# Log-sum-exp over heads: four batches share a turn and logarithm, two more another; one warming matmul per half unit; the last turn in another PSUM bank; the bias check read from the bias row

## The chip, the cores and the metric

The kernel runs on one core of one Trainium2 chip. The metric is the time of one execution on the device in microseconds; the median of three runs counts. A core has five engines with queues of their own: TensorE (PE in the profile, its weight loads PEld), VectorE (DVE), ScalarE (ACT), GpSimd (POOL) and SyncE (SP), which here issues nearly all transfers. Sixteen DMA engines move the data of all queues.

## The reference, cut to what matters

```python
def reference(x, bias):                       # x 8 x 2048 x 2048, bias 8 x 256
    B, S, D = x.shape
    H = bias.shape[0]
    Dh = D // H
    x_heads = x.reshape(B, S, H, Dh).transpose(0, 2, 1, 3)
    x_heads = x_heads + bias[None, :, None, :]
    x_tiled = np.repeat(x_heads, 2, axis=2)   # each row twice
    mx = x_tiled.max(axis=-1, keepdims=True)
    lse = mx.squeeze(-1) + np.log(np.exp(x_tiled - mx).sum(axis=-1))
    return lse.astype(np.float32)             # 8 x 8 x 4096
```

For each of 8 x 2048 rows and each of 8 heads of 256 columns, the bias is added, and the logarithm of the sum of the exponentials is written twice. The input has 134 MB, the output 1 MB.

## The kernel before

**Tiles.** A tile t (0 to 63, eight for each batch) is 256 rows: 128 partitions times K = 2 rows of 2048 columns, 2 MB. Eight tile buffers (`xts`, in pairs `xbs`) hold x and are overwritten in place. Loads go out from SP: tiles 2 to 41 in pairs (4 MB, line 180), the others one by one or, from tile 57 on, by half units of one row per partition (line 192). The last tile's two half units are loaded in column pieces (`LAST_COLS`): the second one as 0-512, 768-1280, 1280-1792, 512-768 and 1792-2048. A load waits until the last users (`last_uses`) of its buffer's earlier tile are done.

**The sums.** No maximum is taken: exp(x + bias) is summed as it stands. The heads of a tile are shared among the engines by the tile's stage (`STAGES`). In the bulk (tiles 0 to 53), the bias of heads 0 to 2 is put into PSUM by `put_bias` (line 312), x is added with an identity matmul (`late_heads`, line 371), and ACT takes the exponential from PSUM (lines 382 and 389); for the heads 4 to 7 POOL adds the bias in place (`g_add`, line 421) and ACT takes the exponential (line 427); head 3 gets its bias as a factor exp(bias) from DVE (line 439); DVE sums (line 446). From tile 57 on, ACT takes the exponential of x as it lands (line 427), DVE multiplies by exp(bias) and sums in one instruction (`weigh`, line 462), POOL folds one or two heads (lines 478 and 486) for a short DVE sum (line 492), and PE and ACT do one to three heads with the bias in PSUM (`put_bias` line 329, `add_x` line 347, `sum_biased` line 402). In each of these half units, 14 in all, `keep_warm` issues `NWARM` = 3 identity matmuls of 128 columns into `tp` (line 362).

**The bias for PE.** `put_bias` uses three matmuls with one row each (`bparts`) for the first `NEARLY` = 5 tiles, and one matmul with `b3`, which holds the parts in three partitions, for later ones. `b3` is filled by three small DMAs that ACT issues (line 239). `first_factors`, `other_factors` and lines 244 to 254 prepare the factors.

**The results.** The sums of batch b lie in a tile `Rx[b]` of 128 partitions with one column before and one behind for a running minimum and maximum. When a batch of the first six is done (two tiles later), `finish(b)` turns its sums with four PE transposes into the PSUM tile `tp` (line 506), and one ACT instruction takes the logarithm, twice per row, into `res` (line 516, 32 partitions). `ends_of(b)` lets DVE carry the smallest and largest sum on to the next tile `Rx[b + 1]` (lines 534 and 537). Behind tile 61 (`t == T - 3`), `turn_two` turns batch 6 into `tp` (line 618), and `store` issues one DMA with the results of the first six batches (line 520). Behind the last tile `finish_two` takes batch 6's logarithm (line 629) and stores it (line 630); `finish_last` turns batch 7 into another quarter of `tp` (line 637), takes the logarithm (line 643) and stores it (line 644). `tp` is one PSUM bank, and the framework keeps writes and reads of two engines in it apart.

**The check.** `b_far` is the largest absolute bias; past a limit, or where a sum has run out of range, `judge` (lines 553 to 562) gives a number that lets all engines branch into `all_again`, a slow exact version that does not run here. `begin_row` (line 547) and `judge` use a row of the PSUM tile `one_ps`.

**Order.** The order on each engine is that in which the program is written (`manual_schedule`); `for_pool` and `for_pe` hold work back for the next unit. Semaphores come from the framework, which derives waits from the operands; `on_x` and `on_bank` declare pairs that need none. DMA completions use a small set of semaphores in turn, so that an issue on SP can also wait for the landing of an earlier DMA.

Of the kernel before, what the change touches and what calls it, by code (L numbers as in the profile page):

```python
# [9 lines left out]
F32 = mybir.dt.float32  # L10
BF16 = mybir.dt.bfloat16
I32 = mybir.dt.int32
ACT = mybir.ActivationFunctionType
# [7 lines left out]

NBUF = 8

NEARLY = 5

NWARM = 3

# [27 lines left out]
    [(0, 512), (1280, 2048), (512, 1280)],  # L57
    [(0, 512), (768, 1280), (1280, 1792), (512, 768), (1792, 2048)],
]


@with_exitstack
def kernel(
# [35 lines left out]
    bparts = sb.tile([1, 3, CPE], BF16, name="bparts")  # L99
    brest = sb.tile([1, 2, CPE], F32, name="brest")  # L100

    b8 = sb.tile([H, Dh], F32, name="b8")
    b_far = sb.tile([H, 1], F32, name="b_far")
    ident_bf = sb.tile([P, P], BF16, name="ident_bf")
    one_bits = sb.tile([1, 1], BF16, name="one_bits")
    ends = sb.tile([P, 2], F32, name="ends")
# [2 lines left out]

    NR = KB * H * NB  # L110

    Rx = [sb.tile([P, 1 + NR + 1], F32, name=f"R{b}") for b in range(B)]
    R = [r[:, 1 : 1 + NR].rearrange("p (k h n) -> p k h n", k=KB, h=H) for r in Rx[:-2]]
    R.append(Rx[-2][:, 1 : 1 + NR].rearrange("p (k h n) -> p k h n", k=K, h=H))
    R_last = Rx[-1][:, 1 : 1 + NR].rearrange("p (h n k) -> p h n k", h=H, n=NBLK)
    res = sb.tile([H * NB, B - 2, P, KB, 2], F32, name="res")
    res_two = sb.tile([H * NBLK, P, K, 2], F32, name="res_two")
    res_last = sb.tile([P, P, 2], F32, name="res_last")
    xbs = [sb.tile([P, KB, D], F32, name=f"xb{i}") for i in range(NBUF // TB)]
# [12 lines left out]
    def pieces(t):  # L132

        if len(modes_of(t)) == 1:
            return [(0, K, 0, D)]
        cols = [[(0, D)]] * K if t < T - 1 else LAST_COLS
        return [(k, k + 1, c0, c1) for k in range(K) for c0, c1 in cols[k]]
# [35 lines left out]
    def load(t):  # L173
        if TB <= t < BLOCKS:

            if t % TB == 0:
                after = [u for i in range(TB) if t >= NBUF for u in last_uses[t + i - NBUF]]
                ins = on_x(
                    t,
                    nc.sync.dma_start(  # L180
                        out=xbs[t // TB % len(xbs)], in_=rows_of(t, TB)
                    ),
                    after,
                )
                for i in range(TB):
                    loads[t + i, 0, 0] = ins
            return
        after = last_uses[t - NBUF] if t >= NBUF else []
        for k0, k1, c0, c1 in pieces(t):
            loads[t, k0, c0] = on_x(  # L190
                t,
                nc.sync.dma_start(
                    out=xts[t % NBUF][:, k0:k1, c0:c1],
                    in_=rows_of(t)[:, k0:k1, c0:c1],
                ),
                after,
            )
# [21 lines left out]
            )  # L219
            break  # L220
    nc.scalar.dma_start(out=brow, in_=bias.rearrange("h j -> (h j)").unsqueeze(0))
    nc.scalar.dma_start(out=b8, in_=bias)
    for t in range(NBUF):
        load(t)
    nc.vector.memset(ones, 1.0)
# [22 lines left out]
    for i, c in enumerate(range(G0, D, MM)):  # L248
# [5 lines left out]
    nc.scalar.activation(out=w_late, in_=w_late, func=ACT.Exp)  # L254

    nc.vector.memset(Rx[0][:, 0:1], 1.0)
    nc.vector.memset(Rx[0][:, 1 + NR :], 1.0)
    nc.vector.memset(one_bits, float(ONE_BITS))
    nc.vector.tensor_reduce(
        out=b_far,  # L260
        in_=b8,
        op=ALU.max,
        axis=mybir.AxisListType.X,
        apply_absolute_value=True,
    )
    nc.vector.tensor_scalar(
        out=Rx[0][0:H, 1 + NR :],
        in0=b_far,
        scalar1=BIAS_MAX,
        scalar2=TOO_FAR,  # L270
# [87 lines left out]
        return heads  # L358

    def keep_warm():  # L360
        for _ in range(NWARM):
            nc.tensor.matmul(  # L362
                tp[:, 0], lhsT=ident, rhs=ident, start=True, stop=True
            )

    def late_heads(m, t, got, sums):

# [131 lines left out]

        return add_fold  # L500

    def finish(b):

        nr = H * NB
        for k in range(KB):
            nc.tensor.transpose(
                out=tp[0:nr, k],
                in_=R[b][:, k].rearrange("p h n -> p (h n)"),
                identity=ident,
            )  # L510
        tv = bass.AP(
            tensor=tp.tensor,
            offset=tp.offset,
            ap=[[tp.ap[0][0], nr], [1, P], [P, KB], [0, 2]],
        )
        nc.scalar.activation(out=res[:, b], in_=tv, func=ACT.Ln)  # L516

    def store():

        nc.sync.dma_start(  # L520
            out=out[0 : B - 2].rearrange("b h (n r) -> (h n) b r", n=NB),
            in_=res.rearrange("q b p k r -> q b (p k r)"),
        )

    def ends_of(b):


        bits = Rx[b].bitcast(I32)
        if b < B - 1:
            low = Rx[b + 1][:, 0:1].bitcast(I32)  # L530
            high = Rx[b + 1][:, 1 + NR :].bitcast(I32)
        else:
            low, high = ends[:, 0:1], ends[:, 1:2]
        nc.vector.tensor_reduce(
            out=high, in_=bits[:, 1:], op=ALU.max, axis=mybir.AxisListType.X
        )
        nc.vector.tensor_reduce(
            out=low,
            in_=bits[:, 0 : 1 + NR],
            op=ALU.min,  # L540
            axis=mybir.AxisListType.X,
            negate=b == B - 1,
        )

    def begin_row():
# [87 lines left out]
        )  # L633

    def finish_last():
        last = tp[:, KB - 1]
        nc.tensor.transpose(
            out=last, in_=R_last.rearrange("p h n k -> p (h n k)"), identity=ident
        )
        tv = bass.AP(  # L640
            tensor=last.tensor, offset=last.offset, ap=[last.ap[0], [1, P], [0, 2]]
        )
        nc.scalar.activation(out=res_last, in_=tv, func=ACT.Ln)
        nc.sync.dma_start(
            out=out[B - 1].rearrange("h (n r) -> (h n) r", r=2 * P),
            in_=res_last.rearrange("q p r -> q (p r)"),
        )
# [25 lines left out]
    def flush(later_work):  # L673
        for f in later_work:
            f()
        later_work.clear()

    for t in range(T):
        if t == T_FACTORS:
            other_factors()  # L680
        xt = xts[t % NBUF]
        sums = sums_of(t)
        for k0, k1, c0, c1 in pieces(t):
            m = modes_of(t)[k0]
            add = None
            heads = []
            if c0 == 0:
                bias_here = bias_there
            if m["late"]:
                pe_part = late_heads(m, t, bias_here, sums)  # L690
            else:
                heads = add_x(m, t, k0, c0, c1, bias_here)

                def pe_part(t=t, heads=heads, sums=sums):
                    for k, h, bank, p, mm in heads:
                        sum_biased(t, k, h, bank, p, mm, sums)

            if c0 == 0:
                if next_units and not m["late"]:
                    bias_there = put_bias(*next_units.pop(0))  # L700
                if t > T_PROMPT and m["g0"] == H:
                    keep_warm()
                if m["g0"] < H:
                    add = g_add(m, t, k0, k1)
                if t < T - 1 or k0 == 0:
                    flush(for_pool)
            h0 = max(c0 // Dh, m["pe"])
            h1 = min(c1 // Dh, m["g0"])
            hf = max(h0, min(h1, H - m["fold"]))
            if h0 < h1 and not m["late"]:  # L710
                done = exp_inplace(
                    t, xt[:, k0:k1, h0 * Dh : h1 * Dh], loads[t, k0, c0]
                )
                if hf < h1:
                    for_pool.append(fold(t, k0, hf, h1, sums, done))
            if c0 == 0:
                flush(for_pe)
            if not m["late"]:
                for k in range(k0, k1):
                    for h in range(h0, hf):  # L720
                        weigh(
                            t,
                            xt[:, k, h * Dh : (h + 1) * Dh],
                            h,
                            sums[:, k, h : h + 1],
                            done,
                        )

            def pool_part(t=t, m=m, k0=k0, k1=k1, sums=sums, add=add):
                if add:  # L730
                    later(m, t, k0, k1, sums, add)
                if k1 == K:
                    reload(t)

            for_pool.append(pool_part)
            if m["g0"] < H:
                pe_part()
                if t == T_PROMPT - 1:
                    first_factors()
                if m["late"]:  # L740
                    bias_there = put_bias(*next_units.pop(0))
            elif heads:
                for_pe.append(pe_part)

        fb, at = divmod(t - 2, NBLK)
        if 0 <= fb < B - 2 and at == NBLK - 1:
            finish(fb)
            ends_of(fb)
        if t == T - 3:
            turn_two()  # L750
            ends_of(B - 2)
            store()
    row = begin_row()
    flush(for_pe)
    flush(for_pool)
    finish_two()
    finish_last()
    ends_of(B - 1)
    again = judge(row) > SPAN_BITS

    order.__exit__(None, None, None)
# [32 lines left out]
```

## Time and profile before

| what | value |
|---|---|
| median of 3 runs | 326.29 us (326.26 to 326.46) |
| the profiled execution | 326.43 us, of which the span from first to last instruction is 324.5 us |
| busy share of the span | PE 77%, DVE 89%, ACT 82%, POOL 89% |
| x queue (q1), share of 16 DMA engines | 98.3% |
| HBM read, written | 134.23 MB, 1.05 MB |
| mean TensorE clock granted | 0.945 of full speed |

Shares are averages over stages that have different limits, so the stretches of time are to be read one by one. The times of lines come from one execution, which took 0.14 us more than the median.

### The profile page before, as it was taken

What the parts mean: (1) busy time and instruction counts of PE and PEld (TensorE: products, weight loads), DVE (VectorE), ACT (ScalarE), POOL (GpSimd) and SP (SyncE); (2) the same over time, 40 slices, a digit from 0 to 9 for tenths busy, and PEclk for the clock granted to TensorE, in tenths of its full rate; (3) what the DMA queues carried; (4) which work ended last, traced back from release to release, by engine and by line L of the source; (5) the groups of instructions that cost most, each with busy time, mean ns of one, the idle gap of its engine ahead of it and who ended that gap; (6) DMA issues with size and microseconds to landing.
All of it is one profiled execution on the core that took longest, in us unless ns stands there. A gap on an engine that the chain in (4) does not pass through costs nothing.

```text
span 324.5 us, 2454 instructions
## 1 busy us (share of the span) xinstructions
PE 250.7 (77%) x691; PEld 106.4 (33%) x691; DVE 287.9 (89%) x330; ACT 266.6 (82%) x426; POOL 287.9 (89%) x121
## 2 busy tenths in 40 slices
PE   5999998778776787777697786677778676398883
PEld 2333333333332233332233332233333322155451
DVE  1146679999999999999969999999999999999995
ACT  1157679899779878788869988889988989889995
POOL 7939998999999999999999999999999999958863
PEclk9977789999999899999879999999999999669999
DMA  7999999999999999999999999999999999999994
GB/s 305 469 392 452 448 402 441 440 420 432 440 420 429 434 428 428 444 424 421 448 421 422 444 428 420 420 430 432 422 424 429 428 425 426 415 421 418 418 397 133
DMA packets 8896, 135.45 MB, mean 417 GB/s; under 512 B 1065, under 2 KB 1457, under 8 KB 2481
## 3 DMA queue, kind: packets, MB, share of 16 engines
q1 hardware_dynamic: 8768, 135.27, 98.3%
q8 instruction: 5, 0.08, 0.1%
q14 instruction: 9, 0.07, 0.1%
q10 hardware_dynamic: 114, 0.02, 0.0%
HBM read 134.23 MB, written 1.05 MB: 417 GB/s over the span
## 4 chain that ended last, share of the span: by engine, by line
DMA 34%; DVE 26%; PE 16%; POOL 14%; ACT 9%; issue 0%; SPq 0%; DVEq 0%
DMA xb<-in_x_dram 33%; DVE R L446 20%; POOL xb L421 14%; PE pair L371 6%; ACT xb L427 6%; PE one_ps L371 4%; DVE xb L439 3%; PE pair L312 3%; DVE xb L462 2%; PE one_ps L312 1%; PE pair L244 1%; ACT xb L389 1%; DMA brow<-in_bias_dram 1%; ACT xb L382 1%; ACT res L516 0%
## 5 line engine op out<-in xcount | busy, mean ns | idle before, releaser
L421 POOL TENSOR_TENSOR xb<-xb,b_rep 128x2048 f32<-128x2048 f32 x57 | 257.5, 4541 | 21.0 <-DMA xb<-in_x_dram 21.0
L446 DVE TENSOR_REDUCE R<-xb 128x14 f32<-128x3584 f32 (+1 forms) x57 | 216.8, 3803 | 1.9
L427 ACT ACTIVATE xb<-xb 128x2560 f32<-128x2560 f32 (+5 forms) x77 | 157.4, 2055 | 17.7 <-POOL xb L421 17.0
L371 PE MATMUL pair<-xb,ident 128*128 128x512 f32 x216 | 110.3, 636 | 0.0
L371 PE MATMUL one_ps<-xb,ident 128*128 128x512 f32 x108 | 61.0, 648 | 13.8 <-DMA xb<-in_x_dram 13.8
L389 ACT ACTIVATE xb<-pair 128x1024 f32<-128x1024 f32 x54 | 55.4, 1026 | 18.1 <-PE pair L371 18.0
L371 PEld LDWEIGHTS pair<-xb,ident 128*128 128x128 f32 x216 | 44.3, 205 | 57.5 <-issue 57.5
L439 DVE TENSOR_TENSOR xb<-xb,w_ps 128x512 f32<-128x512 f32 x54 | 36.7, 680 | 23.9 <-ACT xb L427 23.9
L312 PE MATMUL one_ps<-b,ones_bf 128*128 128x512 bf16 x49 | 19.0, 387 | 37.9 <-ACT xb L382 37.8
L312 PEld LDWEIGHTS <-ones_bf 128*128 128x128 bf16 (+1 forms) x192 | 18.9, 100 | 89.6 <-issue 80.4
L382 ACT ACTIVATE xb<-one_ps 128x256 f32<-128x256 f32 x108 | 39.8, 377 | 6.3 <-PE one_ps L371 6.3
L347 PE MATMUL pair<-xb,ident 128*128 128x512 f32 (+1 forms) x36 | 20.7, 660 | 12.0 <-DMA xb<-in_x_dram 12.0
L312 PE MATMUL pair<-b,ones_bf 128*128 128x512 bf16 x98 | 29.2, 380 | 0.0
L371 PEld LDWEIGHTS one_ps<-xb,ident 128*128 128x128 f32 x108 | 19.2, 196 | 27.5 <-DMA xb<-in_x_dram 20.3
L462 DVE CUSTOM_DVE_ANT_0 xb<-xb,w_ps 128x256 f32<-128x256 f32 x61 | 22.3, 415 | 0.0
L382 ACT ACTIVATION_READ_ACCUMULATOR xb<-one_ps 128x1 f32 x108 | 22.0, 203 | 0.0
L486 POOL TENSOR_TENSOR xb<-xb 128x128 f32<-128x128 f32 (+3 forms) x39 | 13.9, 356 | 3.1
L478 POOL TENSOR_TENSOR xb<-xb,w_sb 128x256 f32<-128x256 f32 (+1 forms) x13 | 10.1, 774 | 5.4 <-ACT xb L427 5.1
L362 PEld LDWEIGHTS tp<-ident 128*128 128x128 f32 x84 | 12.0, 202 | 4.8 <-issue 4.2
L402 ACT ACTIVATE xb<-pair 128x256 f32<-128x256 f32 x33 | 12.5, 396 | 0.0
L362 PE MATMUL tp<-ident 128*128 128x128 f32 x84 | 12.3, 285 | 0.0
L347 PEld LDWEIGHTS pair<-xb,ident 128*128 128x128 f32 x36 | 5.9, 207 | 17.3 <-DMA xb<-in_x_dram 17.2
(60 smaller groups left out, 91.5 us busy)
## 6 DMA issues: line engine op xcount, KB each, us to landing
xb<-in_x_dram SPq DMA_DIRECT2D x20, 4096.0 KB, 21.5
xb<-in_x_dram SPq DMA_DIRECT2D x17, 2048.0 KB, 22.7
xb<-in_x_dram SPq DMA_DIRECT2D x12, 1024.0 KB, 23.4
xb<-in_x_dram SPq DMA_DIRECT2D x4, 256.0 KB, 13.8
xb<-in_x_dram SPq DMA_DIRECT2D x2, 384.0 KB, 15.9
out_dram<-res SPq DMA_DIRECT2D x1, 768.0 KB, 7.2
xb<-in_x_dram SPq DMA_DIRECT2D x2, 128.0 KB, 6.4
out_dram<-res_two SPq DMA_DIRECT2D x1, 128.0 KB, 2.5
```

The source lines that it names most:

```text
L312: nc.tensor.matmul(p, lhsT=lhsT, rhs=each_row(b, h * Dh, Dh, K), start=i == 0, stop=False,)
L347: mm = nc.tensor.matmul(p, lhsT=ident, rhs=xts[t % NBUF][:, ka:kb, c : c + w], start=False, stop=True,)
L362: nc.tensor.matmul(tp[:, 0], lhsT=ident, rhs=ident, start=True, stop=True)
L371: mm = nc.tensor.matmul(p, lhsT=ident, rhs=xts[t % NBUF][:, :, h * Dh : (h + 1) * Dh], start=False, stop=True,)
L382: act = nc.scalar.activation(out=xts[t % NBUF][:, k, 0:Dh], in_=got[0][:, k * Dh : (k + 1) * Dh], func=ACT.Exp, accum_out=sums[:, k, 0:1],)
L389: act = nc.scalar.activation(out=xts[t % NBUF][:, :, Dh : m["pe"] * Dh].rearrange("p k (h j) -> p h k j", j=Dh), in_=got[-1].rearrange("p ...
L421: add = nc.gpsimd.tensor_tensor(out=v, in0=v, in1=each_row(b_rep, c - G0, D - c, k1 - k0), op=ALU.add)
L427: return on_x(t, nc.scalar.activation(out=v, in_=v, func=ACT.Exp), [after])
L439: mul = nc.vector.tensor_tensor(out=f, in0=f, in1=each_row(w_ps, m["pe"] * Dh - W0, n, k1 - k0), op=ALU.mult,)
L446: red = nc.vector.tensor_reduce(out=sums[:, k0:k1, h0:H], in_=v.rearrange("p k (h j) -> p k h j", j=Dh), op=ALU.add, axis=mybir.AxisListTy ...
L462: ttr = nc.vector.tensor_tensor_reduce(out=v, in0=v, in1=w, scale=1.0, scalar=0.0, op0=ALU.mult, op1=ALU.add, accum_out=dst,)
L486: done = nc.gpsimd.tensor_tensor(out=v[:, :, 0:n], in0=v[:, :, 0:n], in1=v[:, :, n : 2 * n], op=ALU.add)
```

## The change

The results of the first six batches are kept in groups: four batches (128 partitions after the turn) and two (64). `finish(i)`, `ends_of(i)`, `Rx` and `res` now go by group, so that there are two turns of four transposes and two logarithms in place of six each, at tiles 33 and 49; `store` issues one DMA for each group. `keep_warm` is one matmul of 384 columns that reads `b_rep` and writes three quarters of `tp`. `turn_two` moves from tile 61 to behind the last tile's work. `finish_last` uses the next bank of `pairs` in place of a quarter of `tp`. The one-row form of the bias is used for two tiles, not five. `b_far` is taken from the bias row `brow` (1 partition of 2048), and the load of the 8 x 256 copy `b8` is gone. The last half unit's pieces 512-768 and 1792-2048 are loaded by one DMA.

```diff
-NEARLY = 5
-
-NWARM = 3
+NEARLY = 2
+
+WARM = 384
...
+LAST_BOTH = (512, 1792)
...
-    b8 = sb.tile([H, Dh], F32, name="b8")
-    b_far = sb.tile([H, 1], F32, name="b_far")
+    b_far = sb.tile([1, 1], F32, name="b_far")
...
+    starts = [0]
+    while starts[-1] < B - 2:
+        starts.append(min(starts[-1] + P // (H * NB), B - 2))
+    groups = list(zip(starts, starts[1:]))
+    widths = [(b1 - b0) * NR for b0, b1 in groups] + [NR, NR]
...
+            if t == T - 1 and k0 == K - 1 and c0 in LAST_BOTH:
+                if c0 == LAST_BOTH[0]:
+                    both = slice(0, None, (LAST_BOTH[1] - c0) // Dh)
+                    v = [
+                        a[:, k0, c0:D].rearrange("p (a j) -> p a j", j=Dh)[:, both]
+                        for a in (xts[t % NBUF], rows_of(t))
+                    ]
+                    ins = on_x(t, nc.sync.dma_start(out=v[0], in_=v[1]), after)
+                    for c in LAST_BOTH:
+                        loads[t, k0, c] = ins
+                continue
...
-    nc.scalar.dma_start(out=b8, in_=bias)
...
         out=b_far,
-        in_=b8,
+        in_=brow,
         op=ALU.max,
...
     def keep_warm():
-        for _ in range(NWARM):
-            nc.tensor.matmul(
-                tp[:, 0], lhsT=ident, rhs=ident, start=True, stop=True
-            )
+        nc.tensor.matmul(
+            tp[:, 0 : WARM // P], lhsT=ident, rhs=b_rep[:, 0:WARM], start=True, stop=True
+        )
...
-    def finish(b):
-
-        nr = H * NB
+    def finish(i):
+
+        nr = widths[i] // KB
         for k in range(KB):
             nc.tensor.transpose(
                 out=tp[0:nr, k],
-                in_=R[b][:, k].rearrange("p h n -> p (h n)"),
+                in_=sums_in[i][:, k * nr : (k + 1) * nr],
                 identity=ident,
             )
...
-        nc.scalar.activation(out=res[:, b], in_=tv, func=ACT.Ln)
+        nc.scalar.activation(out=res[i], in_=tv, func=ACT.Ln)
...
-        nc.sync.dma_start(
-            out=out[0 : B - 2].rearrange("b h (n r) -> (h n) b r", n=NB),
-            in_=res.rearrange("q b p k r -> q b (p k r)"),
-        )
+        for (b0, b1), r in zip(groups, res):
+            nc.sync.dma_start(
+                out=out[b0:b1].rearrange("b h (n r) -> (b h n) r", n=NB),
+                in_=r.rearrange("q p k r -> q (p k r)"),
+            )
...
     def finish_last():
-        last = tp[:, KB - 1]
-        nc.tensor.transpose(
+        bank = n_ps[0] % len(ps)
+        last = ps[bank][:, 0:P]
+        turn = nc.tensor.transpose(
             out=last, in_=R_last.rearrange("p h n k -> p (h n k)"), identity=ident
         )
+        on_bank(bank, turn)
...
-        nc.scalar.activation(out=res_last, in_=tv, func=ACT.Ln)
+        on_bank(bank, nc.scalar.activation(out=res_last, in_=tv, func=ACT.Ln))
...
-        fb, at = divmod(t - 2, NBLK)
-        if 0 <= fb < B - 2 and at == NBLK - 1:
-            finish(fb)
-            ends_of(fb)
+        for i, (_, b1) in enumerate(groups):
+            if t - 2 == b1 * NBLK - 1:
+                finish(i)
+                ends_of(i)
         if t == T - 3:
-            turn_two()
-            ends_of(B - 2)
+            ends_of(len(groups))
             store()
     row = begin_row()
     flush(for_pe)
     flush(for_pool)
+    turn_two()
     finish_two()
     finish_last()
-    ends_of(B - 1)
+    ends_of(len(groups) + 1)
     again = judge(row) > SPAN_BITS
```

## The prediction

> **What bounds the kernel now.** I read the page's slices and queues first, then busy time by stretches, then the chain of waits and the timeline of the last ten microseconds. All lines are of the kernel before.
>
> The page, slices and queues (the digits are tenths in 40 slices):
>
> ```profile
> DMA  7999999999999999999999999999999999999994
> ...
> q1 hardware_dynamic: 8768, 135.27, 98.3%
> ```
>
> The x queue keeps the 16 DMA engines busy from the second slice to the last but one. Is that so even where engines are full? Busy time by stretches:
>
> ```profile
> core 0: us, PE busy (x) PEld busy (x) DVE busy (x) ACT busy (x) POOL busy (x), PEclk, DMA share, GB/s
> 250.00:290.00 40.00, 27.63 (x68) 10.79 (x67) 39.79 (x48) 35.91 (x52) 35.74 (x8) 0.87 1.01 424
> 290.00:300.00 10.00, 8.69 (x44) 5.52 (x42) 10.00 (x49) 10.00 (x22) 8.09 (x18) 1.00 1.01 417
> 300.00:310.00 10.00, 8.15 (x38) 4.95 (x38) 10.00 (x61) 9.79 (x25) 8.21 (x19) 1.00 1.01 419
> 310.00:318.00 8.00, 6.61 (x37) 4.81 (x38) 7.29 (x44) 7.60 (x19) 5.96 (x14) 1.00 1.03 386
> ```
>
> DVE and ACT are full, yet the DMA share is 1.0; earlier stretches of 50 us are alike (424 to 434 GB/s). The page's issues land 21.5 to 23.4 us after their issue, so some 9 MB is always queued (22 us by 424 GB/s). A buffer given back a few us earlier or later changes nothing. Up to about 310 us the stream sets the time, and work taken from PE, ACT or DVE there is worth nothing. Then comes the tail. The chain of waits, in order of time:
>
> ```profile
> 292.89 19.93 DMA xb<-in_x_dram
> ...
> 312.85 1.71 ACT xb L427
> ...
> 319.91 0.14 DVE R L492
> ```
>
> The row of tile 62 that lands at 312.82 starts a DVE run that ends at 320.05. What follows shows in the timeline, and the one wait of SP's at the end:
>
> ```profile
> 319.77 0.60 ACT L629 ACTIVATE res_two<-tp 64x512 f32<-64x512 f32 x1
> 320.39 0.55 SPq L630 DMA_DIRECT2D out_dram<-res_two  x1
> 320.42 0.33 PE L637 MATMUL tp<-ident,R 128*128 128x128 f32 x1 [1.73 <-ACT res_two L629]
> 320.78 0.38 ACT L643 ACTIVATE res_last<-tp 128x256 f32<-128x256 f32 x1 [0.42 <-PE tp L637]
> 321.19 0.36 SPq L644 DMA_DIRECT2D out_dram<-res_last  x1
> ```
> ```profile
> SPq L789 <- DMA out_dram<-res_last: 0.5, 1, 0.5
> ```
>
> The last turn waits for the other logarithm's read of the same bank, not only for its sums (320.05). The last store lands 2.0 us after its issue (the page's issues list), at 323.2; SP had been waiting 0.5 us for it, since 322.7, when the check's branch was through. From 323.2 to the end at 324.5 nothing but closing semaphores runs.
>
> **The change part by part.** *Last turn in another bank.* Its sums are there at 320.05; with the 0.05 us that the chain shows from DVE to a next engine it runs 320.10 to 320.43. ACT is through with res_two at 320.37, so the last logarithm starts at 320.46 (320.78 is 0.03 behind the turn's end now) and ends at 320.84. SP could issue at 320.87, but its issue of res_two holds it from 320.39 to 320.94. So 320.94 for 321.19: 0.25 us earlier, landing at 322.94. Ends: 0, if the two stores (landing 2.5 and 2.0 us after issue) now hold each other up by as much, or if the turn still waits for ACT; 0.50, where SP's own arrival at 322.7 takes over. I take 0.25. The page "DMA: Bandwidth & Descriptors" of the Trainium skill (section Anatomy of one DMA) puts some 2.0 us of a transfer down to setup and receipt; an estimate from its fit is 2.3 us for 128 KB, within what the two stores show, and it leaves the sum as it is.
>
> *Two last loads in one.* The pieces were issued at 310.31 and 312.84 and landed so:
>
> ```profile
> xb<-in_x_dram SPq DMA_DIRECT2D x1, 128.0 KB, 7.5
> ...
> xb<-in_x_dram SPq DMA_DIRECT2D x1, 128.0 KB, 5.3
> ```
>
> That is 317.8 and 318.1. The bytes keep their place in the queue, so both columns now count as landed at 318.1. The first piece's matmul (0.70 us, x2, line 347) moves from 317.85 to 318.2 and ends at 318.9; ACT reads it at 319.41 behind other work. The last piece's exponential starts at about 318.4 behind others anyway. So nothing, with 0.5 us of cover. One issue (0.33 us) leaves SP.
>
> *Turn of batch 6 moved* behind the last matmul and line 547 (0.21 us): two transposes of 0.27 us, 319.1 to about 319.65, and the logarithm that reads them starts at 319.77, when ACT gets to it. Nothing, with 0.1 us of cover; without it 0 to 0.3 us, which passes to the end through ACT. Behind it on PE stand only the last turn (free at 320.10) and the check's matmul (320.88).
>
> *Stores.* Two issues (0.35 us each) for one; with the load that is gone SP has as many as before, at 312.84 and about 313.5, behind all loads in the same queue. SP then sat 5.9 us before line 630. Nothing.
>
> *Warming.* Three pairs of 128 columns took 0.83 us per half unit. A pair of 256 takes 0.70, one of 512 takes 1.02 to 1.13 (line 347), so 384 lies between, about 0.9: +0.07 us, bounds -0.13 and +0.30, in 14 half units of some 2.5 us each, of which PE is busy about 2.0. Covered by DMA; in the last one by the wait for the landing at 318.1. What it may do to the clock is a rival.
>
> *Shared turns and logarithms.* ACT loses four of six (1.01 us each, a width that does not change) and waits of 0.6 us (3.7 over six): 6.5 us. PE loses 16 of 24 transposes (0.27 us): 4.4. DVE goes from 8 pairs of end reductions (0.19 us each in the chain) to 4, of 514, 258, 130 and 130 columns; by line 446 (3.89 us for 3584 columns, 1.09 ns each) a 385-column rise adds 0.41 us and 129 add 0.14: 16 x 0.19 = 3.0 becomes 2.6. All before 256 us but the same last pairs, under a DMA share of 1.0: nothing. PE's transposes at tile 33 wait for DVE with the bulk's matmuls behind them, as each finish did (1.2 us at most).
>
> *One-row bias for two tiles.* Nine matmuls (2.0 us) become three (0.38 each) for three tiles: 2.7 us of PE between 23 and 43 us. b3's last DMA is issued at 9.0 and lands within 6.9 us, before 16; its first reader comes at 23.5. Nothing: the queue behind is full.
>
> *Check from the row.* The reduction goes from 0.40 us to that of 2048 elements (2.28 us at line 446), 8.6 to 10.9 us; DVE then idles until 20.4. Even if ACT's line 254 (now 9.54) waits for it, line 382 behind it needs ACT only at 14.66. ACT loses one 0.29 us issue. Nothing.
>
> Sum: -0.25 us on the profiled execution's own 326.43 us, 326.18; the median of the runs is 0.14 lower, so 326.04. A measurement of this kernel can tell about 0.2%, 0.65 us, from no change.
>
> **Rivals.** *A, slower: the joined load waits for the pieces it steps over.* It writes 512-768 and 1792-2048, and pieces 768-1280 and 1280-1792 between are in flight. If the wait is derived from the whole stretch, SP issues it only when the later one has landed (307.81 + 9.6 = 317.4), and it lands 2.0 to 2.5 us later by the rows of the stores on an emptied queue: 319.4 to 319.9, not 318.1. Then matmul 0.70 and exponential 0.65: ACT reaches res_two at 320.8 to 321.3, not 319.77, so +1.0 to 1.5 us less the 0.25: 327.0 to 327.3. It decides once the landing is later than 318.6. For: two DMAs of one tile, where no declared exemption applies. Against: the columns are disjoint, and nothing before shows such a wait.
>
> *B, slower: the tail's PE clock drops.* The granted clock by stretches of 3.41 us:
>
> ```profile
> 272.34:275.75 3.41, 1.44 (x4) 0.40 (x3) 3.41 (x1) 3.38 (x3) 3.04 (x2) 1.00 0.97 413
> 275.76:279.17 3.41, 1.24 (x3) 0.40 (x3) 3.38 (x3) 2.93 (x6) 3.04 (x2) 0.95 0.99 413
> 279.17:282.58 3.41, 0.41 (x1) 0.00 (x0) 3.41 (x14) 2.52 (x7) 3.32 (x1) 0.50 1.02 423
> ...
> 309.89:313.30 3.41, 1.98 (x12) 1.54 (x12) 2.98 (x18) 3.01 (x8) 2.38 (x6) 1.00 1.00 394
> ```
>
> PE busy for 1.24 us of 3.41 was followed by half clock; 1.44 was not. The tail's emptiest stretch has 1.98, and the new instruction shifts that by tenths; but four of nine weight loads per half unit go. At half clock a half unit's 2.0 us of PE would be up to 4 against a pace of 2.5: one or two units late by 1.5 each, part of it hidden by DVE's run: 327.0 to 328.5. "TensorE: Matmul & The Clock Gate" of the Trainium skill (HAM oscillation) asks for an idle gap of over some 3.4 us before the clock drops; the trace disagrees, since it fell with matmuls in the window. By that rule B could not happen, and the sum would stand.
>
> *C, faster: the engines' lag sets the end.* For: DVE at 10.00 of 10 from 290 to 310. Against: after 310 DVE and ACT wait on landings again. Price: DVE's 0.4 and at most one ACT logarithm (1.01) with the 0.25: 324.8 to 325.6.
>
> *D: the stream runs at another rate*, because tiles lie elsewhere and engines touch memory less. For: with the queue full the stretches still differ by 2% (424 to 434). Against: no load before 310 us is touched. 0.3% of 310 us is 0.9: 325.1, or 327.0 the other way.
>
> **How the numbers follow.** The forecast (with the turn's gain anywhere from 0 to 0.5 and up to 0.3 lost on batch 6's turn) has 0.60; its own range is 325.7 to 326.6. A has 0.10, B 0.05, C 0.08, D 0.14 faster and 0.03 slower. Faster 0.22, within 0.2% 0.60, slower 0.18. The range 325.1 to 327.2 leaves out B, a part of A and the far ends of C and D, some 0.15.
>
> **What would show it.** Right: the last turn starts at about 320.1 behind DVE and no longer behind res_two; the last store is issued at 320.9; its landing ends the run; line 516 appears twice; x's share stays 98%. Wrong: a joined load issued after 313 or landing after 318.6 (A), a clock under 1.00 between 290 and 320 (B), or tile 62's last row landing over 0.3 us away from 312.8 (D).

## The result, and the profile after

The changed kernel takes 325.55 us (median of 14 runs, 325.44 to 326.0), the kernel before in the same session 326.48 us (14 runs, 326.26 to 326.8): 0.93 us faster by the medians; the ratio of the runs is 0.9974 with a 95% interval of 0.9967 to 0.9981. The profiled execution has a span of 323.7 us for 324.5. The forecast was 326.04 us; the result lies inside the range (325.1 to 327.2), 0.15 us below the forecast's own range.

The x queue of the kernel after (the DMA row of the slices has the same digits as before):

```profile
q1 hardware_dynamic: 8768, 135.27, 98.4%
```

Busy time by stretches, the same stretches as before:

```profile
250.00:290.00 40.00, 28.37 (x65) 10.56 (x64) 39.79 (x50) 36.18 (x52) 35.60 (x8) 0.87 1.00 423
290.00:300.00 10.00, 8.03 (x21) 3.10 (x20) 10.00 (x50) 10.00 (x22) 8.34 (x19) 1.00 1.01 419
300.00:310.00 10.00, 7.89 (x21) 3.07 (x21) 10.00 (x60) 9.58 (x26) 8.17 (x19) 1.00 1.01 419
310.00:318.00 8.00, 6.75 (x21) 3.24 (x22) 7.36 (x44) 7.93 (x19) 6.09 (x13) 1.00 0.98 377
```

Little is different to the eye: the queue is full, DVE and ACT are nearly full from 290 to 310 us, the clock is 1.00 from 290 to 318 us. The chain of waits:

```profile
292.58 19.82 DMA xb<-in_x_dram
...
312.42 1.71 ACT xb L450
...
319.48 0.14 DVE R L515
```

Line 450 is what was 427, 515 what was 492. The last row of tile 62 lands at 312.40, 0.42 us earlier than before. The timeline behind it, and SP's waits from 319 us on (nothing else is listed there):

```profile
319.34 0.60 ACT L654 ACTIVATE res_two<-tp 64x512 f32<-64x512 f32 x1
319.76 0.30 PE L663 MATMUL pair<-ident,R 128*128 128x128 f32 x1 [0.84 <-DVE R L515]
319.96 0.47 SPq L655 DMA_DIRECT2D out_dram<-res_two  x1
320.10 0.38 ACT L670 ACTIVATE res_last<-pair 128x256 f32<-128x256 f32 x1 [0.16 <-PE pair L663]
320.53 0.53 SPq L671 DMA_DIRECT2D out_dram<-res_last  x1
```
```profile
SPq L816 <- PEq L816: 0.6, 2, 0.4
```

The last turn now waits for DVE and not for ACT, as planned. SP's wait for the last store, 0.5 us before, is gone from the list. The difference of the two profiled spans (324.54 and 323.71 us), cut at two points:

| stretch | before | after | difference |
|---|---|---|---|
| to the landing of tile 62's last row | 312.82 | 312.40 | -0.42 |
| from there to the last store's issue | 8.37 | 8.13 | -0.24 |
| from the last store's issue to the end of the span | 3.35 | 3.18 | -0.17 |

From here on, the closing is the last row: the time from the last store's issue to the end of the span. Only the middle row was forecast. Two questions are left: why does a stream that was full before end earlier, and what shortens the closing?

### The profile page after: what moved, and what is told of

Same layout as the page of the kernel before. It is cut to its first block, busy times and chain, and to the rows that moved or that the text cites. A ratio compares the mean times of both kernels' runs of the same rounds, so it can differ in the third digit from the quotient of the medians.

```text
span 323.7 us, 2260 instructions
## 1 busy us (share of the span) xinstructions
PE 246.1 (76%) x600; PEld 98.3 (30%) x601; DVE 289.7 (89%) x322; ACT 264.3 (82%) x422; POOL 287.0 (89%) x121
## 4 chain that ended last, share of the span: by engine, by line
DMA 58%; POOL 18%; ACT 11%; DVE 8%; PE 3%; SPq 0%; issue 0%; DVEq 0%
DMA xb<-in_x_dram 58%; POOL xb L444 18%; ACT xb L450 8%; DVE R L469 5%; PE pair L394 2%; DVE xb L485 2%; ACT xb L412 1%; PE one_ps L394 1%; ACT xb L405 1%; DVE xb L462 1%; ACT res L539 0%; SPq L217 0%; ACT xb L425 0%; SPq L194 0%; PE tp L529 0%
## 5 line engine op out<-in xcount | busy, mean ns | idle before, releaser
L394 PE MATMUL pair<-xb,ident 128*128 128x512 f32 x216 | 108.9, 629 | 0.0
L394 PE MATMUL one_ps<-xb,ident 128*128 128x512 f32 x108 | 63.4, 672 | 20.1 <-DMA xb<-in_x_dram 20.1
L336 PE MATMUL one_ps<-b,ones_bf 128*128 128x512 bf16 x52 | 19.9, 382 | 37.7 <-ACT xb L405 37.7
L336 PEld LDWEIGHTS <-ones_bf 128*128 128x128 bf16 (+1 forms) x174 | 17.4, 100 | 85.4 <-issue 78.7
L336 PE MATMUL pair<-b,ones_bf 128*128 128x512 bf16 x104 | 31.0, 379 | 0.0
L371 PE MATMUL pair<-xb,ident 128*128 128x512 f32 (+1 forms) x36 | 21.6, 686 | 12.3 <-DMA xb<-in_x_dram 12.3
L385 PE MATMUL tp<-b_rep,ident 128*128 128x384 f32 x28 | 11.5, 494 | 0.0
L485 DVE CUSTOM_DVE_ANT_0 xb<-xb,one_ps 128x256 f32<-128x256 f32 x27 | 10.6, 412 | 0.6 <-ACT xb L450 0.6
```

Source lines behind the costliest of these rows:

```text
L336: nc.tensor.matmul(p, lhsT=lhsT, rhs=each_row(b, h * Dh, Dh, K), start=i == 0, stop=False,)
L371: mm = nc.tensor.matmul(p, lhsT=ident, rhs=xts[t % NBUF][:, ka:kb, c : c + w], start=False, stop=True,)
L394: mm = nc.tensor.matmul(p, lhsT=ident, rhs=xts[t % NBUF][:, :, h * Dh : (h + 1) * Dh], start=False, stop=True,)
L485: ttr = nc.vector.tensor_tensor_reduce(out=v, in0=v, in1=w, scale=1.0, scalar=0.0, op0=ALU.mult, op1=ALU.add, accum_out=dst,)
```

## Experiments

**How the stream was compared.** From the packets of the x queue in each trace I added up the bytes moved until a given time and divided the difference from the kernel before by 425 GB/s: the stream's lead in us. Differences in the first 5 us are those from one start to the next; what grows after that is rate. "Place" is where the x buffers start in a partition, modulo 512 bytes, from the sizes of the tiles in front of them.

| kernel | place | lead at 5 | 50 | 100 | 200 | 310 us | last row of tile 62 |
|---|---|---|---|---|---|---|---|
| before | 32 | 0 | 0 | 0 | 0 | 0 | 312.82 |
| after | 416 | -0.10 | 0.00 | 0.04 | 0.14 | 0.49 | 312.40 |
| last turn's bank alone | 32 | 0.04 | 0.04 | 0.04 | 0.04 | 0.04 | 312.79 |
| warming alone | 32 | 0.02 | 0.02 | 0.02 | 0.02 | 0.05 | 312.82 |
| head alone | 32 | 0.06 | 0.09 | 0.10 | 0.10 | 0.10 | 312.64 |
| joined load alone | 32 | 0.05 | 0.06 | 0.06 | 0.06 | 0.06 | 312.85 |
| one DMA more | 32 | 0.06 | -0.02 | 0.01 | 0.00 | 0.01 | 312.96 |
| shared logarithms alone | 416 | 0.03 | 0.08 | 0.13 | 0.24 | 0.50 | |
| the same at the old place | 32 | 0.02 | 0.02 | 0.02 | 0.02 | 0.02 | 312.83 |
| before, moved by 896 bytes | 416 | 0.05 | 0.12 | 0.16 | 0.27 | 0.53 | 312.49 |
| before, moved by 32 bytes | 64 | 0.09 | 0.14 | 0.18 | 0.27 | 0.49 | 312.37 |
| before, moved by 992 bytes | 0 | 0.08 | 0.19 | 0.41 | 0.88 | 2.04 | |
| before, moved by 480 bytes | 0 | 0.01 | 0.11 | 0.34 | 0.81 | 1.97 | |
| after, at a multiple of 1024 | 0 | 0.04 | 0.17 | 0.40 | 0.87 | 2.11 | |

An empty last column: the chain of that kernel does not pass the landing. Each row is one trace. The six other kernels at place 32 lead by 0.01 to 0.10 us at the end, so a lead of a tenth says nothing. All times below are medians, against runs of the kernel before on the same chip.

### The parts one by one

*Last turn in another bank:*

```diff
-        last = tp[:, KB - 1]
+        bank = n_ps[0] % len(ps)
+        last = ps[bank][:, 0:P]
```

> The kernel before with one part of the change alone: the last turn in another PSUM bank. The prediction's sum: 0.25 us faster, with the last store issued 0.25 us earlier against the landing of tile 62's last row, and that landing unmoved at about 312.8 us. Theory S (another part of the change makes the x stream itself faster, and that is the other two thirds of the measured 0.93 us): the same 0.25 here, not more. Theory B (the bank alone is the whole gain, by way of the closing of the program): about 0.9 us faster.

326.32 us against 326.38: ratio 0.9998 (0.9989 to 1.0007), no change. The timeline shows why; the third line is from the DMA issues:

```profile
320.17 0.30 PE L638 MATMUL pair<-ident,R 128*128 128x128 f32 x1 [1.50 <-DVE R L492]
...
321.00 0.52 SPq L646 DMA_DIRECT2D out_dram<-res_last  x1
...
out_dram<-res_last SPq DMA_DIRECT2D x1, 128.0 KB, 2.2
```

The turn is 0.25 us earlier, and the store is issued 0.19 earlier, but issuing takes 0.52 us for 0.36 and landing 2.2 for 2.0: it comes down at 323.2, where it did before. The two stores are now 0.64 us apart and were 0.80; that they hold each other up is read from this. From its issue to the end it takes 3.49 us instead of 3.35.

*Warming by one matmul, turn of batch 6 at the end:*

```diff
-        for _ in range(NWARM):
-            nc.tensor.matmul(tp[:, 0], lhsT=ident, rhs=ident, start=True, stop=True)
+        nc.tensor.matmul(
+            tp[:, 0 : WARM // P], lhsT=ident, rhs=b_rep[:, 0:WARM], start=True, stop=True
+        )
...
         if t == T - 3:
-            turn_two()
...
     flush(for_pool)
+    turn_two()
```

> The kernel before with one warming matmul of 384 columns for three of 128, and, since it writes the columns where batch 6's turn lay, that turn behind the last tile. The prediction's sum: 0, within 0.1 us. Theory S with the warming as its cause (from 124 to 130 MB of the stream, where the warming runs, the changed kernel was 0.2 us faster than before): 0.2 to 0.4 us faster, with tile 62's last row landing 0.2 to 0.4 earlier.

326.31 us against 326.38, ratio 1.0002 (0.9993 to 1.0011): nothing, as forecast. The stream's lead is 0.02 to 0.05; the clock is 1.00 from 290 to 318 us, as before.

*Shared turns and logarithms, two result stores* (groups, `finish`, `ends_of` and `store` as in the change):

> The kernel before with the shared turns and logarithms, wider sum tiles, the smaller result tiles and two result stores for one. The prediction's sum: 0. Theory S with this as its cause (fewer instructions and less PSUM and memory traffic through the bulk, another placing of the tiles, and a store spread over 128 partitions): 0.2 to 0.6 us faster, with the stream gaining slowly from tile 16 on and tile 62's last row landing earlier.

325.64 us against 326.38, ratio 0.9979 (0.9970 to 0.9988): most of the gain, where the sum had 0. The lead grows to 0.50 us. The first of the six turns in the kernel before comes at 63 us, and the lead is 0.08 at 50 us already; that hints that it is not the work that is gone, but the head alone, whose stream does not gain, has 0.09 there too. The test is further down, with the buffers at their old place.

*The head: one-row bias for two tiles, check from the row, no 8 x 256 load:*

```diff
-NEARLY = 5
+NEARLY = 2
...
-    nc.scalar.dma_start(out=b8, in_=bias)
...
-        in_=b8,
+        in_=brow,
```

> The kernel before with the head's changes alone: one-row bias for two tiles in place of five, the bias check from the row, no 8 x 256 load. The prediction's sum: 0. Theory S with the head as its cause (the chain of waits before runs through PE until 42 us, and the chain after does not): 0.2 to 0.6 us faster, all of it in the landing of tile 62's last row, and gained before about 60 us.

325.99 us against 326.38, ratio 0.9990 (0.9981 to 0.9999). Not by the way expected: the stream has a lead of 0.06 at 5 us and 0.10 from 100 us on, which is how far traces differ, and no more. The span is 0.54 us shorter: 0.18 of that is the earlier landing of tile 62's last row, and 0.36 lie behind the last store's issue (2.99 us to the end for 3.35).

*The joined load:*

```diff
+            if t == T - 1 and k0 == K - 1 and c0 in LAST_BOTH:
+                if c0 == LAST_BOTH[0]:
...
+                    ins = on_x(t, nc.sync.dma_start(out=v[0], in_=v[1]), after)
```

> The kernel before with one part of the change alone: the last half unit's pieces 512-768 and 1792-2048 in one load. The prediction's sum: 0. Rival A (the joined load waits for the pieces it steps over): 0.9 us slower or more. Theory L (at the end SP waits for one DMA semaphore after the other, DMAs take the semaphores in turn, and the number of DMAs issued decides whether the last store's semaphore is the first waited for or a later one; in the kernel before it is the first, and 0.5 us are waited there): one DMA less, as in the kernel with the head's changes, so 0.2 to 0.4 us faster, with tile 62's last row landing where it did and no wait on the last store in front of SP's first closing event.

326.02 us against 326.31, ratio 0.9988 (0.9979 to 0.9997). The load goes out at 310.34 and waits for no neighbour: rival A falls. The chain, the last issue and SP's waits at the end:

```profile
292.84 20.02 DMA xb<-in_x_dram
...
321.22 0.36 SPq L658 DMA_DIRECT2D out_dram<-res_last  x1
...
SPq L803 <- PEq L803: 0.6, 2, 0.4
```

All is where it was until 321.22, even 0.03 us later. But no wait for the last store stands in front of SP's closing, and the span ends 2.98 us behind the issue, not 3.35.

### What the stream's lead comes from

*The kernel before, the x buffers moved* (only `res_last`, which lies in front of them, is longer):

```diff
-    res_last = sb.tile([P, P, 2], F32, name="res_last")
+    res_last = sb.tile([P, P + 112, 2], F32, name="res_last")[:, 0:P]
```

> The kernel before with one result tile made 896 bytes longer per partition, so that the tile buffers of x, which lie behind it, move by 896 bytes; nothing else changes. The x buffers then start at byte 928 of a 1024-byte stretch, as they do in the kernel with the shared logarithms alone, and not at byte 32. Theory M (the x stream's gain comes from where its buffers lie in a partition): the stream gains 0.4 to 0.5 us by its end, the kernel 0.4 to 0.8 us. Theory I (it comes from the turns, logarithms and end reductions that are gone): no change, within 0.1 us.

325.96 us against 326.32, ratio 0.9988 (0.9979 to 0.9997). Not one instruction was added or taken, and the lead runs beside that of the shared logarithms: 0.53 and 0.50 at 310 us. The kernel gains 0.36, a little under the 0.4 that was expected.

> As before, moved by 32 bytes, so that the x buffers start at a multiple of 64 bytes, which they do in none of the kernels so far. Theory M with the offset within 64 bytes as the cause: a change of the stream by some tenths of a us or more, faster. Theory M with a longer stretch as the cause, or theory I: no change, within 0.1 us.

325.94 us, ratio 0.9990 (0.9981 to 0.9999): a lead of 0.49. A multiple of 64 is no better than byte 416, but byte 32 is worse than both; why is not shown.

> As before, moved by 992 bytes, so that the x buffers start at a multiple of 1024 bytes. Theory M with alignment as the cause: at least the gain of the move by 896 bytes, 0.4 us or more. Theory I: no change, within 0.1 us.

324.35 us (6 runs, 323.9 to 325.77), ratio 0.9944 (0.9928 to 0.9960): a lead of 2.04, 2.0 us off the time. Busy time by stretches of this kernel:

```profile
250.00:290.00 40.00, 28.93 (x80) 11.63 (x79) 39.79 (x54) 36.59 (x53) 35.68 (x10) 0.87 1.01 428
290.00:300.00 10.00, 7.91 (x37) 4.76 (x36) 10.00 (x50) 10.00 (x26) 8.75 (x22) 1.00 1.01 425
```

The same share of busy DMA moves 428 and 425 GB/s where 424 and 417 went before. In the trace the packets take less time: those of 8192 bytes take 315.2 ns on the mean at byte 32, 314.3 at byte 64, 314.5 at 416 and 309.6 here; those of 3072 bytes 126.2 and 121.0, and the most frequent ones, of 32768 bytes, 1218.8 and 1214.2. So the gain is 4 to 6 ns for each packet, whatever its size. Summed over the 6656 packets of 3072, 8192, 16384 and 32768 bytes and shared among 16 engines it is 1.9 us, nearly all of the lead.

*The shared logarithms with the x buffers at their old place* (the longer tile is 16512 bytes):

> The kernel before with the shared turns and logarithms alone, and a result tile made longer by 16512 bytes per partition, so that the x buffers lie exactly where they lie in the kernel before. Theory M: the stream's lead of 0.5 us is gone, and no more than 0.2 us of the 0.74 us that the shared logarithms gave is left. Theory I: 0.7 us faster, as without the longer tile.

326.09 us against 326.32, ratio 0.9992 (0.9984 to 1.0001). The lead is 0.02 at 310 us. So of the 0.74 us that this part gave, 0.51 are the place of the buffers (0.74 less the 0.23 that are left), and the turns, logarithms and end reductions gave the stream nothing. What is left is a little over the 0.2 that was expected at most; it lies behind the last store's issue, 3.10 us for 3.35. Theory M holds, theory I falls.

*512 or 1024 bytes:*

> As the moves by 896, 32 and 992 bytes: the x buffers of the kernel before moved by 480 bytes, to byte 512 of a 1024-byte stretch. Theory M with 512 bytes as the stretch that counts: as with the move by 992 bytes, the stream 2.0 us faster and the kernel 1.8 to 2.1. With 1024 bytes as the stretch: 0.4 us, as for bytes 64 and 928.

324.14 us (6 runs) against 326.31, ratio 0.9939 (0.9922 to 0.9956), lead 1.97: a multiple of 512 does as well as one of 1024. Whether 128 or 256 would do was not tried. The Trainium skill has a rule near this: "DMA: Bandwidth & Descriptors", section How a descriptor splits into AXI transactions, says that a descriptor which does not start at a multiple of 256 bytes begins with a transaction from the boundary below, of which the bytes before the start are fetched unused and cost beats. The runs agree in that bytes 32, 64 and 416, all off a multiple of 256, are slower than byte 0. They do not agree in the order: by the rule byte 32 has the fewest unused bytes of the three, and it is the slowest. The rule also speaks of what is read, and here it is the start of the tile that a load writes which moved.

### What shortens the closing

*One DMA more:*

```diff
     nc.scalar.dma_start(out=b8, in_=bias)
+    nc.scalar.dma_start(out=b8_more, in_=bias)
```

> The kernel before with one DMA more: the 8 x 256 bias is loaded a second time at the start, to a tile that lies behind all others and that nothing reads. Nothing else moves. Theory L: the last store takes another semaphore, as in the kernel with the shared logarithms alone, which has one DMA more too, so 0.1 to 0.4 us faster, all of it behind the last store's issue. If the number of DMAs does not matter: no change, or slower by up to 0.1 us.

326.32 us against 326.31, ratio 1.0002 (0.9993 to 1.0011): no change, where 0.1 to 0.4 us was expected. SP's wait at the end:

```profile
SPq L791 <- DMA out_dram<-res_last: 0.3, 1, 0.3
```

The wait shrinks from 0.5 to 0.3 us and the closing from 3.35 to 3.24, but the last row of tile 62 landed 0.14 later, and the end is where it was.

What SP does there can be read from its wait instructions in the traces. When the check's branch is through, it asks for the eight semaphores of the DMAs one after the other, always in the same order; where nothing holds it, each comes 0.06 to 0.09 us behind the one before. The DMAs take these semaphores in turn, so their number decides which of the eight the last store has:

| kernel | the last store's semaphore | store landed | SP is past it | end of the span |
|---|---|---|---|---|
| before | first | 323.21 | 323.22 | 324.54 |
| one DMA more | second | | 323.32 | 324.56 |
| shared logarithms at the old place | second | | 323.05 | 324.29 |
| joined load | eighth | 323.21 | 323.35 | 324.20 |
| head | eighth | 323.02 | 323.14 | 324.00 |
| after | eighth | 322.65 | 322.86 | 323.71 |

(Where the column is empty, the trace does not tell the landing.) The rows before and joined load settle it: the store lands at 323.21 in both. Before, SP stands at the first semaphore until then and has seven to go; with one DMA less it has passed the seven in the meantime, and the span ends 0.33 us earlier. So theory L's mechanism is shown. Its number for one DMA more was too high: the second place saves one step, less than a tenth. The last store has the first semaphore also with the bank alone, with the warming alone and in the kernels moved by 896, 32, 992 and 480 bytes. In the last of these it was issued 1.4 us behind the other store and landed in 1.7, before SP asked for it, so nothing was waited there. Of the two kernels with the second place, one has a closing of 3.10 and the other of 3.24, because SP is past the store 1.85 and 2.00 us after its issue; why the one lands sooner is not shown.

Where the last store is the eighth, it had landed 0.12 to 0.24 us before SP asked for it (four kernels). Then its landing does not end the run. The end hangs on the check: SP reads the verdict, branches and asks for the eight semaphores. From the start of that reading to the end it takes 2.57 to 2.64 us in the six kernels without a wait for the store, and 2.93 before.

### A faster version

*The changed kernel with the x buffers at a multiple of 1024 bytes* (`res_last` 96 bytes longer):

> The changed kernel with a result tile made 96 bytes longer per partition, so that the x buffers start at a multiple of 1024 bytes. Theory M: the stream, which in the changed kernel led that of before by 0.5 us, leads by 2.0, and the time falls from 0.93 us below before to 2.3 to 2.6 us below it, 323.8 to 324.1 us. If the two gains have one cause in part that is not the place: less than 2.0 us below before.

323.57 us (5 runs, 323.48 to 324.55) against 326.31: ratio 0.9923 (0.9910 to 0.9936). That is 2.7 us below before, a little more than expected; the changed kernel was 0.93 below it in its own session, so the place adds 1.8. Here the stream no longer sets the tail. The chain of waits from 280 us on, by line:

```profile
by line: DVE xb L485 68.9%; DVE R L469 15.7%; DVE R L515 3.1%; DVE R L485 1.7%; DVE ends L559 0.7%; DVE verdict L587 0.7%; PE one_ps L586 0.5%; DVE ends L562 0.5%; DVE R L559 0.5%; DVE R L562 0.5%; DVE far L578 0.4%; issue 0.4%; DVEq L559 0
```

From 280 us to the end it runs through DVE, which has 10.00 of 10 busy from 280 to 310; no DMA is left in it. That was rival C, and it comes true once the stream is 2 us faster.

## Why the prediction was right or wrong

**The bound.** Right: the x stream sets the time up to 310 us. Taking PE, ACT and DVE work out of that stretch gave the stream nothing, as the shared logarithms at the old place show.

**The step that failed: "under a DMA share of 1.0: nothing".** A share of 1.0 says that the DMA engines are busy and not how fast they are. The shared logarithms free 16.5 thousand bytes per partition in front of the x buffers, which moves these from byte 32 of a 512-byte stretch to byte 416, and the stream gains 0.5 us over the run: the move alone, with no instruction changed, gives the same. How it gains is shown in part. Packets of 32768 bytes take 1217.6 ns in place of 1218.8, but summed over the four sizes above the shorter packets make only 0.2 to 0.4 us of the 0.5 in the four kernels at 416 and 64. The prediction had this as rival D, "because tiles lie elsewhere", with 0.14 for the faster side, and priced it at 0.9 us from 0.3% of 310 us; it is half that. That one can work out the place from the tile sizes before the run was overlooked. It named the sign by which D would show, tile 62's last row over 0.3 us away from 312.8; it came 0.42 earlier.

**Last turn's bank, the only term of the sum.** The steps up to the issue held: the turn at DVE's end, the issue 0.24 us earlier against tile 62's landing. The step that failed is that the last store's "landing ends the run". Alone the bank brought 0.06 us, with the interval on both sides of none: the two stores hold each other up, which was the prediction's lower end, and it took the middle. In the whole change the last store has the eighth semaphore; it lands at 322.65, and SP asks for it at 322.86. What ends the run there is the check's verdict on DVE:

```profile
321.14 0.28 DVE L562 TENSOR_REDUCE verdict<-one_ps 1x1 int32<-1x128 f32 x1 [0.31 <-PE one_ps L561]
...
320.71 0.28 DVE L587 TENSOR_REDUCE verdict<-one_ps 1x1 int32<-1x128 f32 x1 [0.31 <-PE one_ps L586]
```

The first line is of the kernel before, the second of the kernel after. Cut along this path, the two spans differ so:

| stretch | before | after | difference |
|---|---|---|---|
| to the end of the verdict | 321.42 | 320.99 | -0.43 |
| from there to SP's reading of it | 0.19 | 0.12 | -0.07 |
| from there to the end of the span | 2.93 | 2.61 | -0.32 |

The first row is the stream, the third the semaphore. SP reads the verdict 0.05 us after it has issued the last store, so an earlier issue can have given the second row and no more. The fit from which the prediction estimated 2.3 us for a store is given in the Trainium skill, "DMA: Bandwidth & Descriptors", section Anatomy of one DMA, for transfers that GpSimd issues; these go out from SP, and took 2.0 to 2.5 us.

**Joined load, and the load of the bias copy.** Costed at nothing, on the ground that their bytes and their waits move nothing. That is so for the stream, but each made the closing nearly 0.4 us shorter (3.35 to 2.98 and 2.99), because with one DMA less the last store has the last of the semaphores that SP asks for. The prediction had read this wait, 0.5 us, and asked only when the store lands.

**Why the parts don't add up.** Alone they give 0.06, 0.07, 0.74, 0.39 and 0.29 us, together 1.55; the change gives 0.93. The shorter closing is in three of them and can be had once.

**How much of it was luck.** The measured 325.55 us lies inside the stated range, but the way there was not the forecast one. Of the two things that made the gain, the stream's rate stood in the prediction as a rival, and the semaphores did not stand in it at all; the one term of the sum gave at most 0.07 us. The range held because it was wide enough for rival D.

**Zeros that held.** Warming: 0.81 us a pair (forecast 0.9). Batch 6's turn ran 318.51 to 318.92, its logarithm at 319.34. Joined load landed at 317.7, issued at 309.92. The clock is 1.00 from 290 to 318 us, so rival B did not come. The row on which B's price rests is weaker than it was taken: before the clock fell at 278.82, PE had been idle from 274.36 to 277.93, for 3.57 us, so that drop alone does not speak against a rule of idle gaps. Another drop of the same trace does, at 159.36: no idle stretch of PE before it is longer than 1.7 us, and PE was busy for 1.55 us of the 3.41 us before it, more than the 1.44 that were taken as safe.

## What to carry to other kernels

Where a profile shows a load stream with a full queue, look at what one packet takes, and put the buffers at a multiple of 512 bytes in the partition: 480 or 992 unused bytes did more here than the whole change. When a part that should be worth nothing moves the time, keep its instructions and put the buffers back where they were, before looking for a cause in the work. Before pricing an earlier last store, ask whether its landing ends the run, or another chain that ends beside it. Parts that shorten the same wait can be had once, so their gains measured alone do not add up.

## What the runs showed of the hardware

- A packet of 8192 bytes loaded into one partition took 315.2 ns of a DMA engine when the x buffers started 32 bytes past a multiple of 512, 314.2 to 314.5 at 64 and 416, and 309.6 at a multiple of 512. Packets of 32768 bytes took 1218.8 and 1214.2 ns at 32 and 0, so the difference is per packet and not per byte.
- Two stores of 128 KB issued 0.64 us apart took 2.5 and 2.2 us to land, and the second's issue 0.52 us of SP; 0.80 us apart they took 2.5 and 2.0, and 0.36.
- At the program's end SP asked for its eight DMA semaphores in a fixed order, 0.06 to 0.09 us apart. A last store that landed at 323.21 us let the span end at 324.54 when it had the first of them and at 324.20 when it had the eighth; one DMA less in the program made that difference.
